# Reciprocal RMS by way of DRAM to all partitions, and the kernel's head written as a function of its own, in a decoder layer on one core

## The chip, the core and the metric

The kernel runs on one core of a Trainium2 chip, as one program. The metric is the device time in microseconds of one execution, the median over runs. A core has TensorE (PE, matmuls; PEld is its weight load), VectorE (DVE), ScalarE (ACT), GpSimd (POOL) and SyncE (SP), each with an instruction stream of its own. DMAs are issued from such a stream and then run on 16 DMA engines. SBUF and PSUM have 128 partitions.

## The reference

One decoder layer over a sequence of 2048 tokens of 1024 features, in float32, cut here to what the change touches:

```python
def rmsnorm(x, w, eps=EPS):
    inv = lax.rsqrt(jnp.mean(x * x, axis=-1, keepdims=True) + eps)   # one number per token
    return x * inv * w

def reference(x, ...):
    proj = rmsnorm(x, norm_mix_w) @ w_in      # k, v, q of attention; f, q, v, g of 4 gated linear-attention heads
    ...                                       # attention in a window of 128 with sinks; chunked recurrence
    h = x + mix @ w_out
    a = rmsnorm(h, norm_ffn_w)
    y = silu(causal_conv(a @ w_gate)) * (a @ w_up)     # 2816 channels
    return rmsnorm(h + y @ w_down, final_norm_w)
```

The inverse 1/rms is one number for each token. It commutes with the matmul, so the kernel multiplies it into the results, not into the input.

## The kernel before

Features lie on partitions and tokens along the free dimension. P is 128, KT = 8 tiles make up the 1024 features, and the sequence is worked in NH = 2 halves of HALF = 1024 tokens. Every float32 matmul is done as three fp32r matmuls of high and low parts (XH by whi, XL by whi, XH by wlo); ACT makes the high part and DVE the low one, for activations (`split`, L215) and weights (`prep`, L177). A `unit` (L190) is one 128-row block of a projection: 8 tiles by 3 products by 2 blocks of 512 tokens, 48 matmuls of 128 x 512 into two PSUM banks. The pool `mm` has four such banks, the pools `hg` and `at` two each.

The stages of a half are: load x and make its parts (`load`, L275); two units `kv` for keys and values (`first_unit`, L306); the unit `f` of the first head; four times a recurrence head (`hgrn`, L433, beginning with its unit `hq`) and an attention head (`attend`, L343), where `att_keys` (L312) multiplies `kv` by the inverse; the output projection (`out_proj`, L646); gate and up in 11 pairs of blocks (`gate_up`, L838), each as seven products of a fast 2 x 2 matrix multiplication with operands S, T and B; and the down projection with the final norm (`down`, L919).

The inverse. `Stats` (L228 on) collects the sum of squares over the feature tiles: ACT squares a tile, DVE adds it to `acc`, 128 x tokens. `inverse` (L243) then sums over partitions with matmuls against a column of ones (`pst`: 8 blocks of 128 tokens, tokens now on partitions) and DVE computes `rs`, 128 x 8, in 13 small steps (`rsqrt`, L155). To have the number of a token on all partitions, `inverse` writes a diagonal matrix (`ident` times `rs`, L253) and `spread` (L257) multiplies it by a matrix of ones (`pinv`, L263, plain f32) and copies the result out of PSUM on ACT (L266). The tile that then holds the inverse is called `invb`, or `sums` for the final norm of half 0. There are nine places: x and h in each half; the final norm of half 0 in two pieces of 512 tokens, s2 and then s1, both worked while half 1's `kv` units run on PE; and that of half 1 in s2 with 512 tokens and two last pieces of 256, whose `pinv` stays in PSUM (`spread(0)`, `spread(1)`).

`finish` (L1089) multiplies eight tiles of the output by the inverse on DVE and stores each. In `gate_up` the inverse of h multiplies the first pair's gate (`ga`, L856), so `then` hangs `hs.inverse` and `hs.spread` on two of that pair's seven products (L865). Behind the multiplies come the convolution (L883, L885) and the next pair's operands.

The head. At the start the first tile of x comes in two parts and the first weight in two column blocks, 128 and 896 wide, with the second weight behind the second tile. The seven small constants are fetched on ACT's queue. PE runs WARM = 12 idle matmuls of ones (L91). Then come `kv` (96 matmuls), the statistics, `f` with the spread hung on its fifth step, and the first `hq`. Loads are issued by SP in program order. The order of instructions on each engine is made by a scheduler, which simulates the program with its own costs and goes by that; program order and the calls of `issue_after` bind it only in part.

Of the kernel before, what the change touches and what calls it, by code (L numbers as in the profile page):

```python
# [13 lines left out]
ALU = mybir.AluOpType  # L14
# [35 lines left out]
def hymba_layer(ctx: ExitStack, tc: tile.TileContext, a: dict, out: bass.AP):  # L50
# [32 lines left out]
    nc.scalar.activation(warm, ones[:, 0:1], AF.Sigmoid)  # L83
# [20 lines left out]
    def constants():  # L104
# [21 lines left out]
        nc.scalar.dma_start(battn, a["b_attn"])  # L126
# [3 lines left out]
        nc.scalar.dma_start(C.hgw, a["hg_norm_w"])  # L130
        C.sinkb = cp.tile([P, ATT_J, 2], F32, name="sinkb")
        nc.scalar.dma_start(C.sinkb.rearrange("p j k -> p (j k)"), a["sinks"].to_broadcast([P, 8]))
        C.nfw = cp.tile([P, KT], F32, name="nfw")
        nc.scalar.dma_start(C.nfw, a["norm_ffn_w"])
        C.fnw = cp.tile([P, KT], F32, name="fnw")
        nc.scalar.dma_start(C.fnw, a["final_norm_w"])
        C.cw = cp.tile([P, FT, 4], F32, name="cw")
        nc.scalar.dma_start(C.cw, a["conv"])

        lbl = cp.tile([P, 2, HG], F32, name="lbl")  # L140
        nc.scalar.dma_start(lbl, a["lb_logits"])
# [35 lines left out]
    def prep(src, slots=False, parts=(slice(0, D),), between=[]):  # L177

        raw = raw4(None)
        hi, lo = [hp.tile([P, D], F32R, tag="m", name=f"w{t}", bufs=KT) if slots else  # L180
                  wp.tile([P, D], F32R, tag=t, name=f"w{t}", bufs=2) for t in ("hi", "lo")]
        for c in parts:
            nc.sync.dma_start(raw[:, c], src[:, c])
            nc.scalar.copy(hi[:, c], raw[:, c])  # L184
            nc.vector.tensor_tensor(lo[:, c], raw[:, c], hi[:, c].bitcast(F32), op=ALU.subtract)  # L185
            if between:
                between.pop(0)()
        return hi, lo

    def unit(src, X, name, order=range(KT), kind="mm", then={}, behind={}, in_turn=False):  # L190
# [5 lines left out]
        for both in [[h] for h in halves()] if in_turn else [halves()]:  # L196
            for i, kt in enumerate(order):
# [6 lines left out]
                with tc.issue_after(mark) if mark else ExitStack():  # L204
                    for w, x, f, l in ((wh, xh, kt == order[0], False), (wh, xl, False, False),
                                       (wl, xh, False, kt == order[-1])):
                        for b, bs in both:
                            nc.tensor.matmul(o[b], w, x[:, bs], start=f, stop=l)  # L208
# [16 lines left out]

    class Stats:


        def __init__(self, acc, sq=None, eng=None, k=0):
            self.acc, self.sq, self.eng, self.k = acc, sq, eng or [nc.vector], k  # L230

        def halves(self):
            n = self.acc.shape[-1] // 2
            return [Stats(self.acc[:, i * n:(i + 1) * n], self.sq, self.eng, self.k) for i in range(2)]

        def add(self, src):
            t = self.acc if self.k == 0 else self.sq()[:, 0:src.shape[-1]] if self.sq else src
            nc.scalar.activation(t, src, AF.Square)
            self.k += 1
            if self.k > 1:  # L240
                return self.eng[(self.k - 1) % len(self.eng)].tensor_tensor(self.acc, self.acc, t, op=ALU.add)

        def inverse(self, keep):  # L243
# [4 lines left out]
            for c in range(nt):  # L248
                nc.tensor.matmul(st[:, c:c + 1], self.acc[:, c * P:(c + 1) * P], ones[:, 0:1],
                                 start=True, stop=True)  # L250
            rs = self.rs = rsqrt(st[:, 0:nt], nt, 1.0 / D, keep)
            dg = self.acc
            return nc.vector.tensor_tensor(dg.rearrange("p (c t) -> p c t", t=P),  # L253
# [3 lines left out]
        def spread(self, bank=None):  # L257

            n = self.acc.shape[-1]
            w = min(n, 512)  # L260
            for b in range(n // w):
                pb = ps(aux[b % 2 if bank is None else bank], "pinv")[:, 0:w]
                nc.tensor.matmul(pb, ones, self.acc[:, b * w:(b + 1) * w], start=True, stop=True)  # L263
                if bank is not None:
                    return pb
                nc.scalar.copy(self.acc[:, b * w:(b + 1) * w], pb)  # L266
# [8 lines left out]
    def load(hf, X, stage, W=None):  # L275

        st = Stats(inv_tile())
        xt = []

        def part(kt, c):  # L280
            nc.sync.dma_start(xt[kt][:, c], a["xT"][kt, :, hf * HALF + c.start:hf * HALF + c.stop])
            split(xt[kt][:, c], nmw[:, kt:kt + 1], dst=[t[:, c] for t in X[kt]])

        for kt in range(KT):
            xt.append(stage())
# [923 lines left out]
```

## Time and profile before

| | us |
|---|---|
| median of 3 runs (2201.37 to 2201.8) | 2201.75 |
| the profiled execution | 2201.32 |
| its span in the profile | 2199.6 |
| PE busy | 2176.4 |
| DVE busy | 1643.6 |
| ACT busy | 1050.3 |
| POOL busy | 6.3 |

Times in the profile are microseconds from the span's start. A row of the timeline has start, duration, engine, line, operation, output<-inputs, shape, and the number of instructions in a group; in brackets stands how long the engine had been idle before it and what it waited for. An f32 matmul of full precision leaves two records on PE. In a table of windows a line has the stretch, its length, then busy time (and instructions) of PE, PEld, DVE, ACT and POOL, the clock that TensorE was granted, the mean busy share of the DMA engines, and what they moved in GB/s.

### The profile page before, as it was taken

What the parts mean: (1) busy time and instruction counts of PE and PEld (TensorE: products, weight loads), DVE (VectorE), ACT (ScalarE), POOL (GpSimd) and SP (SyncE); (2) the same over time, 40 slices, a digit from 0 to 9 for tenths busy, and PEclk for the clock granted to TensorE, in tenths of its full rate; (3) what the DMA queues carried; (4) which work ended last, traced back from release to release, by engine and by line L of the source; (5) the groups of instructions that cost most, each with busy time, mean ns of one, the idle gap of its engine ahead of it and who ended that gap; (6) DMA issues with size and microseconds to landing.
All of it is one profiled execution on the core that took longest, in us unless ns stands there. A gap on an engine that the chain in (4) does not pass through costs nothing.

```text
span 2199.6 us, 29514 instructions
## 1 busy us (share of the span) xinstructions
PE 2176.4 (99%) x11406; PEld 1831.2 (83%) x11406; DVE 1643.6 (75%) x2490; ACT 1050.3 (48%) x1845; POOL 6.3 (0%) x27
## 2 busy tenths in 40 slices
PE   9999999999999999999999999999999999999998
PEld 7988988888888888888889889888888888888887
DVE  6568568688887888875856666577888888887766
ACT  5446454454444445335725455535634444444353
POOL 1000000000000000000000000000000000000000
PEclk9999999999999999999999999999999999999999
DMA  4101112323333234964631111204132323259643
GB/s 154 51 30 50 37 44 68 119 73 104 102 111 106 91 125 144 377 235 162 202 125 49 37 37 50 68 30 139 53 134 87 127 84 120 96 190 392 225 136 130
DMA packets 94214, 257.91 MB, mean 117 GB/s; under 512 B 11578, under 2 KB 17402, under 8 KB 94074
## 3 DMA queue, kind: packets, MB, share of 16 engines
q1 hardware_dynamic: 88128, 251.70, 33.5%
q10 hardware_dynamic: 5946, 4.34, 0.7%
q8 instruction: 89, 1.46, 0.3%
q14 instruction: 51, 0.42, 0.1%
HBM read 195.10 MB, written 57.15 MB: 115 GB/s over the span
## 4 chain that ended last, share of the span: by engine, by line
PE 95%; DVE 3%; DMA 1%; ACT 1%; issue 0%; ACTq 0%; DVEq 0%
PE X L790 7%; PE X L791 7%; PE X L792 7%; PE pop L208 7%; PE hq L208 4%; PE q L208 4%; PE f L208 4%; PE g L208 4%; PE pdx L1001 4%; PE pdx L1003 4%; PE Y L792 4%; PE Y L791 4%; PE Y L790 4%; PE pdx L1002 4%; PE pdy L1003 3%; PE pdy L1001 3%
## 5 line engine op out<-in xcount | busy, mean ns | idle before, releaser
L619 ACT CAST whi<-raw 128x1024 fp32r<-128x1024 f32 x88 | 92.7, 1053 | 109.8 <-PE X L791 67.6
L790 PE MATMUL X<-T,whi 128*128 128x512 f32 x352 | 136.9, 389 | 0.0
L791 PE MATMUL X<-T,whi 128*128 128x512 f32 x352 | 136.9, 389 | 0.0
L792 PE MATMUL X<-T,wlo 128*128 128x512 f32 x352 | 136.9, 389 | 0.0
L885 DVE SCALAR_TENSOR_TENSOR y<-ga,cw,y 128x1024 f32<-128x1024 f32 x88 | 112.4, 1279 | 26.0 <-ACT y L883 25.9
L797 ACT COPY u<-X 128x512 f32<-128x512 f32 x88 | 51.5, 585 | 133.8 <-PE X L792 133.7
L620 DVE TENSOR_TENSOR wlo<-raw,whi 128x1024 fp32r<-128x1024 f32 x88 | 107.1, 1217 | 0.0
L184 ACT CAST whi<-raw 128x1024 fp32r<-128x1024 f32 (+2 forms) x61 | 62.7, 1033 | 81.9 <-PE q L208 31.9
L620 DVE TENSOR_TENSOR xld<-raw,xhd 128x1024 fp32r<-128x1024 f32 x72 | 80.7, 1131 | 19.0 <-ACT xhd L619 18.6
L619 ACT CAST xhd<-raw 128x1024 fp32r<-128x1024 f32 x72 | 69.7, 978 | 42.8 <-DMA raw<-act0T 15.3
L208 PE MATMUL pop<-XL,whi 128*128 128x512 f32 x256 | 85.3, 393 | 2.1 <-DVE XL L220 2.1
L208 PE MATMUL pop<-XH,wlo 128*128 128x512 f32 x256 | 84.6, 391 | 0.8 <-DVE wlo L185 0.8
L208 PE MATMUL pop<-XH,whi 128*128 128x512 f32 x256 | 83.9, 395 | 0.2
L185 DVE TENSOR_TENSOR wlo<-raw,whi 128x1024 fp32r<-128x1024 f32 (+2 forms) x61 | 73.1, 1204 | 8.9 <-ACT whi L184 8.9
L792 PEld LDWEIGHTS X<-T,wlo 128*128 128x128 f32 x352 | 66.1, 188 | 13.7
L791 PEld LDWEIGHTS X<-T,whi 128*128 128x128 f32 x352 | 66.1, 188 | 13.8
L790 PEld LDWEIGHTS X<-T,whi 128*128 128x128 f32 x352 | 66.1, 188 | 13.7
L1001 PE MATMUL pdx<-xhd,hid 128*128 128x512 f32 x192 | 74.4, 391 | 1.2 <-ACT hid L619 1.0
L1002 PE MATMUL pdx<-xld,hid 128*128 128x512 f32 x192 | 74.7, 389 | 0.0
L1003 PE MATMUL pdx<-xhd,lod 128*128 128x512 f32 x192 | 73.7, 389 | 0.0
L611 PE MATMUL pvv<-whi,XH 128*128 128x256 f32 x256 | 73.5, 288 | 0.0
L612 PE MATMUL pvv<-whi,XL 128*128 128x256 f32 x256 | 72.7, 285 | 0.0
(363 smaller groups left out, 6560.8 us busy)
## 6 DMA issues: line engine op xcount, KB each, us to landing
wr<-in_w_down SPq DMA_DIRECT2D x90, 512.0 KB, 5.3
raw<-in_w_gate SPq DMA_DIRECT2D x44, 512.0 KB, 3.6
raw<-in_w_up SPq DMA_DIRECT2D x44, 512.0 KB, 3.6
raw<-act0T SPq DMA_DIRECT2D x20, 512.0 KB, 5.8
raw<-act1T SPq DMA_DIRECT2D x20, 512.0 KB, 10.2
act0B<-y SPq DMA_DIRECT2D x33, 256.0 KB, 2.5
act1B<-y SPq DMA_DIRECT2D x33, 256.0 KB, 2.4
raw<-in_w_out SPq DMA_DIRECT2D x16, 512.0 KB, 4.8
```

Source lines behind the costliest of these rows:

```text
L185: nc.vector.tensor_tensor(lo[:, c], raw[:, c], hi[:, c].bitcast(F32), op=ALU.subtract)
L208: nc.tensor.matmul(o[b], w, x[:, bs], start=f, stop=l)
L611: nc.tensor.matmul(o[:, 0:256], xh[:, t], hi[:, c], start=kt == 0, stop=False)
L619: return (nc.scalar.copy(h, src), (eng or nc.vector).tensor_tensor(l, src, h.bitcast(F32), op=ALU.subtract))
L620: (eng or nc.vector).tensor_tensor(l, src, h.bitcast(F32), op=ALU.subtract))
L790: nc.tensor.matmul(o, wh[:, ws], xh, start=i == 0 and not more, stop=False, skip_group_check=more)
L791: nc.tensor.matmul(o, wh[:, ws], xl, start=False, stop=False, skip_group_check=more)
L792: r = nc.tensor.matmul(o, wl[:, ws], xh, start=False, stop=i == 3, skip_group_check=more)
L885: nc.vector.scalar_tensor_tensor(y, g[:, w:w + HALF], C.cw[:, ft, w:w + 1], y, op0=ALU.mult, op1=ALU.add)
L1001: nc.tensor.matmul(o, wh[:, i, c], ah[:, i, cols], start=f, stop=False, skip_group_check=more)
L1002: nc.tensor.matmul(o, wh[:, i, c], al[:, i, cols], start=False, stop=False, skip_group_check=more)
L1003: nc.tensor.matmul(o, wl[:, i, c], ah[:, i, cols], start=False, stop=l, skip_group_check=more)
```

## The change

Seven of the nine inverses (x and h of both halves, s2 of half 0, s1, and the 512-token s2 of half 1) no longer use the diagonal, the matrix of ones and the copies. `inverse` with `sent` writes `rs` to a row in DRAM by a DMA from ACT's queue, tokens in order, and a second DMA, from POOL's queue, reads that row onto every one of the 128 partitions of `acc`: 1024 or 512 numbers on each. The last two pieces of 256 tokens keep the matrix of ones (`sent=False`).

The head becomes a function. `head` gives ACT's instructions an order (`turn`) and PE's likewise, step by step: `step(u, kt)` is one feature tile of one of the two kv units, six matmuls. The first weight is loaded in column blocks of 128, 384 and 512, the last two from ACT's queue ahead of the warm-up activation, and cast in these blocks; the second is cast in blocks of 256 and 768, and its first two steps come before x's third tile. x's tiles are all requested one behind the other, without a wait for the weights' casts. The constants are fetched from SP's queue, behind the loads of x and of `w_f`. The weights of `f` are cast before the statistics, and `f` stands behind `pst` on PE. The scheduler's order changes as well in the later stages, among them that of the products of the first gate and up pairs.

```diff
+        def inverse(self, keep, sent=True):
 
             n = self.acc.shape[-1]
             nt = n // P
             st = ps("hg", "pst")
             for c in range(nt):
-                nc.tensor.matmul(st[:, c:c + 1], self.acc[:, c * P:(c + 1) * P], ones[:, 0:1],
+                marks["pst"] = nc.tensor.matmul(st[:, c:c + 1], self.acc[:, c * P:(c + 1) * P], ones[:, 0:1],
                                  start=True, stop=True)
             rs = self.rs = rsqrt(st[:, 0:nt], nt, 1.0 / D, keep)
+            if sent:
+                row = dp.tile([nt, P], F32, name=f"row{len(sent_rows)}")
+                sent_rows.append(row)
+                nc.scalar.dma_start(row.rearrange("c p -> p c"), rs)
+                nc.gpsimd.dma_start(self.acc, row.rearrange("c p -> (c p)").unsqueeze(0).to_broadcast([P, n]))
+                return
             dg = self.acc
-            return nc.vector.tensor_tensor(dg.rearrange("p (c t) -> p c t", t=P),
+            nc.vector.tensor_tensor(dg.rearrange("p (c t) -> p c t", t=P),
                                     ident.unsqueeze(1).to_broadcast([P, nt, P]),
                                     rs.unsqueeze(2).to_broadcast([P, nt, P]), op=ALU.mult)
 
-        def spread(self, bank=None):
+        def spread(self, bank):
 
             n = self.acc.shape[-1]
-            w = min(n, 512)
-            for b in range(n // w):
-                pb = ps(aux[b % 2 if bank is None else bank], "pinv")[:, 0:w]
-                nc.tensor.matmul(pb, ones, self.acc[:, b * w:(b + 1) * w], start=True, stop=True)
-                if bank is not None:
-                    return pb
-                nc.scalar.copy(self.acc[:, b * w:(b + 1) * w], pb)
+            pb = ps(aux[bank], "pinv")[:, 0:n]
+            nc.tensor.matmul(pb, ones, self.acc, start=True, stop=True)
+            return pb
...
+    def head(X):
+
+
+        st = Stats(inv_tile())
+        raw = [raw4(None) for _ in range(3)]
+        W = [tuple(wp.tile([P, D], F32R, tag=t, name=f"w{t}", bufs=2) for t in ("hi", "lo")) for _ in range(2)]
+        xt = [slot("x") for _ in range(KT)]
+        k0, k1, k2 = slice(0, P), slice(P, 4 * P), slice(4 * P, D)
+        v0, v1 = slice(0, 2 * P), slice(2 * P, D)
+        nc.sync.dma_start(raw[0][:, k0], a["w_att"][ATT_J][:, k0])
+        for c in (k1, k2):
+            fetched = nc.scalar.dma_start(raw[0][:, c], a["w_att"][ATT_J][:, c])
+        with tc.issue_after(fetched.ins):
+            nc.scalar.activation(warm, ones[:, 0:1], AF.Sigmoid)
+        for kt in range(KT):
+            for c in [h for _, h in halves()] if kt == 0 else [slice(0, HALF)]:
+                nc.sync.dma_start(xt[kt][:, c], a["xT"][kt, :, c])
+            if kt == 1:
+                nc.sync.dma_start(raw[1], a["w_att"][ATT_J + 1])
+        nc.sync.dma_start(raw[2], a["w_f"][0])
+        o = [[ps("mm", f"kv{b}") for b in range(NB)] for _ in range(2)]
+        on_act, on_pe = [], []
+
+        def turn(f, *args):
+
+            with tc.issue_after(on_act[-1].ins) if on_act else ExitStack():
+                on_act.append(f(*args))
+
+        def tile_of_x(kt):
+            X.append(new_x())
+            for c in [h for _, h in halves()] if kt == 0 else [slice(0, HALF)]:
+                turn(split_w, xt[kt][:, c], nmw[:, kt:kt + 1], [t[:, c] for t in X[kt]])
+
+        def split_w(src, w, dst):
+            h, l = dst
+            r = nc.scalar.activation(h, src, AF.Identity, scale=w)
+            nc.vector.scalar_tensor_tensor(l, src, w, h.bitcast(F32), op0=ALU.mult, op1=ALU.subtract)
+            return r
+
+        def step(u, kt):
+
+            hi, lo = [t[:, kt * P:(kt + 1) * P] for t in W[u]]
+            xh, xl = X[kt]
+            with tc.issue_after(on_pe[-1].ins) if on_pe else ExitStack():
+                for w, x, f, l in ((hi, xh, kt == 0, False), (hi, xl, False, False), (lo, xh, False, kt == KT - 1)):
+                    for b, bs in halves():
+                        r = nc.tensor.matmul(o[u][b], w, x[:, bs], start=f, stop=l)
+                on_pe.append(r)
+
+        turn(cut, *W[0], raw[0], k0)
+        tile_of_x(0)
+        step(0, 0)
+        turn(cut, *W[0], raw[0], k1)
+        tile_of_x(1)
+        step(0, 1)
+        turn(cut, *W[0], raw[0], k2)
+        turn(cut, *W[1], raw[1], v0)
+        for kt in range(2):
+            step(1, kt)
+        for kt in range(2, KT):
+            tile_of_x(kt)
+            if kt == 2:
+                turn(cut, *W[1], raw[1], v1)
             else:
-                part(kt, slice(0, HALF))
-            if W is not None and kt == 1:
-                W.append(prep(a["w_att"][ATT_J + 1]))
-
-            if W is None:
-                st.add(xt[kt])
-            elif kt >= 3:
-                st.add(xt[kt - 3])
-            yield st
-        for kt in range(KT - 3, KT) if W is not None else ():
-            st.add(xt[kt])
-
-    def first_unit(X, W, i, then={}):
-        return unit(W[i] if W else a["w_att"][ATT_J + i], X, "kv", then=then)
+                turn(st.square, xt[kt - 3])
+            for u in range(2):
+                step(u, kt)
+        F = tuple(hp.tile([P, D], F32R, tag="m", name=f"w{t}", bufs=KT) for t in ("hi", "lo"))
+        turn(cut, *F, raw[2], slice(0, D))
+        for kt in range(KT - 3, KT):
+            turn(st.square, xt[kt])
+        summed = st.last
+        with tc.issue_after(on_act[-1].ins), tc.issue_after(summed.ins):
+            constants()
+        with tc.issue_after(on_pe[-1].ins):
+            st.inverse("x")
+        with tc.issue_after(marks["pst"].ins):
+            f0 = unit(F, X, "f", kind="aux")
+        return o, st.acc, st.rs, f0, summed
+
+    def first_unit(X, i, then={}):
...
-            then = {"S4": lambda: hs.inverse("h"), "A22": lambda: (hs.spread(), flush())} if pr == 0 else {}
+            then = {"S4": lambda: hs.inverse("h"), "A22": flush} if pr == 0 else {}
...
-                        steps[0][0].inverse("o")
+                        steps[0][0].inverse("o", False)
                     elif i and d == 1:
                         inv = steps[0][0].spread(0)
                     elif i and d == 2:
                         finish(hf, hh, steps[0][0], steps[0][1], [nc.sync], inv)
-            steps[1][0].inverse("o")
+            steps[1][0].inverse("o", False)
             finish(hf, hh, steps[1][0], steps[1][1], [nc.scalar, nc.sync], steps[1][0].spread(1))
             return None
-        kv = [first_unit(X, None, 0, {3: lambda: s1.inverse("o"), 7: lambda: xs.inverse("x")})]
-        kv.append(first_unit(X, None, 1, {2: lambda: (s1.spread(), finish(hf, hh, s1, lo, [nc.sync])), 4: xs.spread}))
+        kv = [first_unit(X, 0, {3: lambda: s1.inverse("o"), 7: lambda: xs.inverse("x")})]
+        kv.append(first_unit(X, 1, {2: lambda: finish(hf, hh, s1, lo, [nc.sync])}))
...
-    X, W = [], []
-    for xs in load(0, X, lambda: slot("x"), W):
-        pass
-    kv = [first_unit(X, W, i) for i in range(2)]
-    constants()
-    xs.inverse("x")
-    f0 = unit(a["w_f"][0], X, "f", kind="aux", then={4: xs.spread})
-    nxt = X, kv, xs.acc, xs.rs, f0
+    X = []
+    *nxt, summed = X, *head(X)
...
-        nc.scalar.dma_start(battn, a["b_attn"])
+        nc.sync.dma_start(battn, a["b_attn"])
-        nc.scalar.dma_start(lbl, a["lb_logits"])
+        nc.sync.dma_start(lbl, a["lb_logits"])
```

More of the change, by code (lines that the diff above doesn't have):

```diff
@@ L272, in slot, with load @@
         return hp.tile([P, HALF], F32, tag="m", name=name, bufs=KT)
[L275 removed]
+    def load(hf, X, stage):
         st = Stats(inv_tile())
[L278 to L282, printed above, removed]
         for kt in range(KT):
[L285 removed]
+            x = stage()
             X.append(new_x())
[L287 to L304 removed]
@@ L1113, in hymba_layer @@
                 at = attend(hf, h, X, invb, KS, V, mix, p)
-                next(hg)
+                with tc.issue_after(summed.ins) if hf + h == 0 else ExitStack():
+                    next(hg)
                 if h == HG - 1:
```

59 lines of the change are left out of this document (30 added, 29 removed).

## The prediction

> **What bounds the kernel now.** I read the page's busy shares first, then the chain that ended last, then the windows by stage.
>
> ```profile
> PE 2176.4 (99%) x11406; PEld 1831.2 (83%) x11406; DVE 1643.6 (75%) x2490; ACT 1050.3 (48%) x1845; POOL 6.3 (0%) x27
> PE 95%; DVE 3%; DMA 1%; ACT 1%; issue 0%; ACTq 0%; DVEq 0%
> 10.00:13.00 3.00, 2.18 (x6) 1.38 (x6) 2.03 (x2) 2.68 (x3) 0.00 (x0) 0.50 1.03 404
> 13.00:16.00 3.00, 3.00 (x9) 2.32 (x8) 2.49 (x4) 3.00 (x4) 0.00 (x0) 0.50 1.03 407
> 17.00:20.00 3.00, 3.00 (x15) 2.48 (x14) 3.00 (x3) 2.97 (x5) 0.00 (x0) 1.00 1.02 407
> 600.00:1100.00 500.00, 499.49 (x2208) 413.35 (x2207) 399.51 (x480) 239.33 (x311) 0.00 (x0) 1.00 0.49 171
> ```
>
> PE is busy 99% of the span and is 95% of the chain. The windows have, after the stretch's length, the busy time of PE, PEld, DVE, ACT and POOL, then the granted clock, the DMA engines' busy share and GB/s. From 600 to 1100 PE idles 0.5 of 500 us, so an instruction taken from PE there shortens the span by its own time, and later work on another engine costs nothing until PE lacks an operand. Only the first 17 us differ: PE has holes, and its granted clock is 0.50 from 10 to 16. So the change has two sides: what it takes from PE, and whether PE must wait for what comes instead. The profiled execution took 2201.32 us (span 2199.6 and 1.72 around it), 0.02% under the median of 2201.75; I sum against 2201.32.
>
> **The ones-matmuls that go.** Beside the tile summary of `pinv` (duration min/median/max), PE's timeline shows what one costs:
>
> ```profile
> L263 PE MATMUL pinv<-invb,ones x22: 379/592/796, 44.9 to 2192.8; 128*128 128x512 f32 x18, 128*128 128x256 f32 x4
> L263 PE MATMUL pinv<-sums,ones x4: 590/590/591, 1102.1 to 1118.4; 128*128 128x512 f32 x4
> 44.02 0.62 PE L208 MATMUL f<-XH,whi 128*128 128x512 f32 x2
> 44.47 0.62 PE L208 MATMUL f<-XL,whi 128*128 128x512 f32 x2
> 44.93 1.88 PE L263 MATMUL pinv<-invb,ones 128*128 128x512 f32 x4
> 46.24 1.04 PE L208 MATMUL f<-XH,wlo 128*128 128x512 f32 x2
> 47.12 0.62 PE L208 MATMUL f<-XH,whi 128*128 128x512 f32 x2
> 48.50 0.39 PE L208 MATMUL hq<-XH,whi 128*128 128x512 f32 x1
> ```
>
> Pairs of matmuls start every 0.45 us (44.02, 44.47), 0.227 each. After the pair at 44.47 the next two should start at 44.93 and 45.38; with four `pinv` records (two matmuls; an f32 one is two records) the second starts at 47.12. So two cost 47.12 − 45.38 = 1.73 us, one 0.87. Of 26 records 22 have 512 columns, which are 11 matmuls: two each for x and h in both halves, and one each for the final norm's s2 of half 0, s1, and s2 of half 1. All 11 go; the last two eighths keep theirs (four records of 256 columns). 11 × 0.87 = **−9.5 us**, all where PE is the chain. The diagonals on DVE and the copies of `pinv` on ACT go too; they lie beside PE and count nothing.
>
> **The new trip.** Now rs goes from ACT's queue to a DRAM row, 1024 or 512 elements of 4 bytes, and from POOL's queue back to 128 partitions, 512 or 256 KB. The second waits for the first. Before has neither, and no DMA on POOL's queue. The nearest rows (issue to landing):
>
> ```profile
> DMA to landing us min/median/max: 1.8/2.5/4.2
> raw<-in_w_gate SPq DMA_DIRECT2D x44, 512.0 KB, 3.6
> wr<-in_w_down SPq DMA_DIRECT2D x90, 512.0 KB, 5.3
> raw<-act1T SPq DMA_DIRECT2D x20, 512.0 KB, 10.2
> ```
>
> The first row is that of `odd<-moved`, a small DMA on ACT's queue. Call L the time from rs to the landed broadcast. It is at least 1.8 + 3.6 = 5.4 and at most 4.2 + 10.2 = 14.4. I take 2.5 + 5.3 = 7.8, say 8: a weight load is nearest in size, and the slower of the weight rows allows for a queue that nothing used before. The Trainium skill's page "DMA: Bandwidth & Descriptors", section "Anatomy of one DMA — SWDGE (gpsimd) path", gives such a DMA 2.0 us plus its bytes at 436 GB/s, an estimated 3.2 us for 512 KB; with the 2.5 in front L would be 5.7, no site below would wait, and the sum would be −12.0. No run here shows a DMA of that queue.
>
> What L may be before PE waits, site by site. **x of half 0:**
>
> ```profile
> 34.02 1.84 PE L249 MATMUL pst<-ones,invb 128*128 128x1 f32 x16
> 38.43 0.17 DVE L168 SCALAR_TENSOR_TENSOR y<-t,y 128x8 f32<-128x8 f32 x1
> 46.60 0.69 DVE L326 TENSOR_TENSOR kT<-kv,invb 128x512 f32<-128x512 f32 x1 [6.67 <-ACT invb L266]
> ```
>
> The key/value units end at 33.8, rs 4.8 later at 38.60; in the new order the last sum of squares comes some 0.5 us later against them, so 5.3. Then PE has pst (1.84) and f, 48 × 0.227 = 10.9, until 12.8 after the units' end. hq then needs a PSUM bank that kT's multiply frees, 0.7 after the landing. PE waits 5.3 + L + 0.7 − 12.8 = L − 6.8: **+1.2 us** at L = 8, nothing up to 6.8, 7.6 at 14.4. The row's DMA also holds ACT until rs is there; behind it stands kT's activation, which needs the inverse anyhow.
>
> **h, twice.** The inverse meets the first gate pair:
>
> ```profile
> 484.71 0.17 DVE L168 SCALAR_TENSOR_TENSOR y<-t,y 128x8 f32<-128x8 f32 x1
> 488.68 2.50 DVE L856 TENSOR_TENSOR ga<-ga,invb 128x512 f32<-128x512 f32 x4 [2.55 <-ACT invb L266]
> 494.90 1.05 ACT L619 CAST Sh<-S 128x1024 fp32r<-128x1024 f32 x1
> 500.56 0.39 PE L790 MATMUL Y<-T,Sh 128*128 128x512 f32 x1
> ```
>
> The multiplies start 3.8 us after rs; behind them on DVE and ACT stand the convolution and the next pair's operands, of which Sh is ready at 495.95 and read at 500.56. That is 4.6 us of slack, less the 1.7 by which PE comes earlier, less 1.2 for Sl's subtract that follows Sh; and in PE's new order 20 more matmuls stand before that read, 4.5 us. PE waits from L = 3.8 + 4.6 − 1.7 − 1.2 + 4.5, about 10: nothing at 8. DVE's new order puts two subtracts (1.9 us) ahead of the multiplies; they fit in its 2.55 us of idle time. On ACT behind the row stand copies of X and Y that wait for PE until 487 anyway, after rs.
>
> **x of half 1, with s1:**
>
> ```profile
> 1112.77 1.22 DVE L253 TENSOR_TENSOR invb<-ident,y 128x1024 f32<-128x1024 f32 x1
> 1122.39 0.39 PE L208 MATMUL f<-XH,whi 128*128 128x512 f32 x1
> 1124.46 1.28 DVE L326 TENSOR_TENSOR kT<-kv,invb 128x512 f32<-128x512 f32 x2
> ```
>
> rs is there at 1112.7. f starts 3 × 0.87 earlier plus the one of s2, near 1119, and ends near 1130: L ≤ 11 is covered (1112.7 + 11 + a multiply of s1 in front and kT's own, some 5, is 1129). Nothing at 8. Behind ACT's row of s1 stands a weight cast, whose load is there long before.
>
> **Tail, s2 of half 1:**
>
> ```profile
> 2163.13 0.16 DVE L168 SCALAR_TENSOR_TENSOR y<-t,y 128x4 f32<-128x4 f32 x1
> 2167.45 4.91 DVE L1092 TENSOR_TENSOR h<-h,invb 128x512 f32<-128x512 f32 x8
> 2172.28 0.41 DVE L987 TENSOR_TENSOR h<-h,pdx 128x256 f32<-128x256 f32 x1
> 2176.70 0.50 PE L249 MATMUL pst<-ones,invb 128*128 128x1 f32 x4
> ```
>
> Eight multiplies of 4.91 stand on DVE ahead of the last sums, of which the pst at 2176.70 needs all. They could start 2163.3 + L instead of 2167.45; the sums behind them take till about 4.9 after that, pst can wait until L ≈ 7.8. **+0.2** at 8. Its row has half the bytes, which is on the safe side. The end (last pst, last `pinv`, four multiplies, store) is untouched.
>
> **The head.** Constants leave ACT's queue for SP's, behind w_f and ahead of the next weights; ACT, DVE and PE get a step order by hand.
>
> ```profile
> 9.41 0.33 ACTq L141 DMA_DIRECT2D lbl<-in_lb_logits  x1
> 32.85 2.00 ACT L184 CAST whi<-raw 128x1024 fp32r<-128x1024 f32 x2 [5.60 <-PE kv L208]
> 7.98 0.49 PE L208 MATMUL kv<-XH,whi 128*128 128x512 f32 x1 [0.36 <-ACT XH L222]
> 9.15 0.60 PE L208 MATMUL kv<-XL,whi 128*128 128x512 f32 x1 [0.68 <-DVE XL L223]
> 9.79 1.15 ACT L222 ACTIVATE XH<-x,nmw 128x1024 fp32r<-128x1024 f32 x1 [0.92 <-DMA sinkb<-in_sinks]
> 10.97 1.28 DVE L223 SCALAR_TENSOR_TENSOR XL<-x,nmw,XH 128x1024 fp32r<-128x1024 f32 x1 [1.88 <-ACT XH L222]
> 10.99 2.16 PE L208 MATMUL kv<-XH,whi 128*128 128x512 f32 x4 [0.82 <-ACT XH L222]
> ```
>
> Seven issues of 0.33 are 2.3 us that SP's later loads wait; those are cast after 33, twenty us after their old issue, so this costs nothing; without that cover it would be the 2.3. Before, ACT sits behind a constant's DMA until 9.79, and PE has its second x tile at 10.99. Played through with the durations above, XH of x1 comes at 8.7, XL at 10.0, the first two tiles are done at 13.6 for both units, and six more take 12 × 0.227 = 2.7 each (DVE's 2.5 per tile fits): units end at 29.9 instead of 33.8, **3.9** less. That is at full clock. A half-clock stretch of 3 us, as from 10 to 13, costs half of it, 1.5; both stretches 3. I count one, **−2.5**, and keep 0.9 to 3.9 as its ends. The Trainium skill, "TensorE: Matmul & The Clock Gate", Part 1, has the clock halve after an idle window of some 3.4 us that runs freely; the trace agrees with a half clock after the holes, for some 6 us. By that rule the gain hangs on where a window falls.
>
> Sum: −9.5 − 2.5 + 1.2 + 0.2 = −10.6, so **2190.7 us**.
>
> **Rivals.** The window of the first site:
>
> ```profile
> 36.00:50.00 14.00, 14.00 (x59) 10.83 (x58) 6.88 (x21) 3.74 (x6) 0.00 (x0) 1.00 0.21 75
> ```
>
> *A slow trip.* As L grows, all sites charge: gain = 12.0 − (L − 6.8) − (L − 7.8) − 2(L − 10) − (L − 11), each bracket from its own zero. At 10 it is 6.6, at 11 2.6, at 11.6 nothing, at 13 −7.4: **2208.7, slower**. It decides from L = 12.5 on, which costs over 0.2% (4.4 us, about what a measurement of this kernel can tell from no change). For it: act1T's 10.2 us, a store of 1024 single elements, 128 reads of one 4 KB row, a queue never seen here. Against it: at these places the DMA engines are idle for 79% of the time from 36 to 50, and the weight loads land in 3.6 to 5.3. I give 0.13, and 0.10 to L from 10.7 to 12.5, which lands within 0.2%.
>
> *POOL's transfer held by DVE.* If its descriptors wait until DVE pauses, it starts later by one DVE instruction, 1.2 to 2.5 us by the subtracts above: L = 10, gain 6.6, **2194.7**. Against it: DVE is idle 6.67 us at the first site, and busy 6.88 of 14 us around it. Chance 0.09. The Trainium skill, "SBUF — State Buffer", section "SBUF: two separate sides", says that a DMA issued from GpSimd starves while DVE runs a two-port fast-mode operation, with 620 ns grown to 3100; no run here shows it.
>
> *The head brings nothing.* The kernel's first tiles come when the loads land, and PE falls into the same half clock. Then units end as before, the waits of 1.4 stay: 2201.32 − 9.5 + 1.4 = **2193.2**. For it: the loads already ran at 404 GB/s from 10 us on. Chance 0.13. That the change does not do what it says would be `pinv` records at 45 us; the new order has none there.
>
> **Numbers.** The forecast (L from 5.4 to 9.5, head 0.9 to 3.9) has 0.55; with the last two rivals faster has **0.77**, same **0.10**, slower **0.13**. Its own range is 2187.9 (12.0 + 1.4 gained, no wait) to 2195. Downward 1.9 more for what the scheduler's new order of the gate and up products may save (the size of those two subtracts); upward I go into the slow trip as far as L ≈ 11.6: 2186 to 2201.3, with some 0.16 above it and 0.04 below.
>
> **What would show it.** Right: no L263-like f32 matmul between 40 and 2170; units ending between 30 and 33; the broadcast landing 7 to 9 us after the last y; PE idle about 1 us before the first hq; the first gate pair without idle PE. Wrong: a broadcast landing over 11 us after rs, with PE idle before hq, before the second gate pair and before the tail's pst; or units ending at 33.8 again at a half clock.

## The result and the profile after

| | us |
|---|---|
| before, median of 5 runs (2200.27 to 2201.8) | 2201.37 |
| changed, median of 5 runs (2238.2 to 2244.3) | 2241.18 |
| ratio, 95% interval | 1.0184, 1.0172 to 1.0195 |
| forecast | 2190.7, 2186.0 to 2201.3 |

The change makes the kernel 39.8 us slower. The changed kernel's page, in the rows that answer to those of before (busy shares, chain), and its two small DMA queues:

```profile
PE 2172.0 (97%) x11384; PEld 1829.2 (82%) x11384; DVE 1636.2 (73%) x2485; ACT 1044.7 (47%) x1836; POOL 9.8 (0%) x34
PE 85%; DMA 6%; DVE 6%; ACT 1%; issue 1%; SPq 0%; DVEq 0%; POOLq 0%; ACTq 0%
q10 hardware_dynamic: 10970, 4.75, 0.8%
q0 software_dynamic: 816, 2.88, 0.4%
```

PE has 22 records fewer, as forecast, and is busy only 4.4 us less; of the span of 2236.3 it idles 64.3 us, against 23.2 of 2199.6 before. DMA has become 6% of the chain. What PE waits for (engine, line, waited for: us, times, longest):

```profile
PE pv L407 <- ACT vT L398: 13.7, 1, 13.7
PE pst L252 <- DVE invb L239: 9.1, 2, 7.0
PE Y L861 <- ACT Sh L690: 8.8, 2, 5.5
PE hq L203 <- DVE kT L397: 7.9, 1, 7.9
```

Those are the forecast's own sites: x of half 1, the tail, the first gate pair of both halves, x of half 0. Here is the earliest of them, x of half 0, in the timeline, then the windows (stretch, length, busy PE, PEld, DVE, ACT, POOL, granted clock, DMA share, GB/s):

```profile
35.81 0.17 DVE L167 SCALAR_TENSOR_TENSOR y<-t,y 128x8 f32<-128x8 f32 x1
36.01 0.39 ACTq L258 DMA_DIRECT2D row<-y  x1
47.25 0.70 POOL L259 DMA_DIRECT2D invb<-row  x1 [40.69 <-DMA row<-y]
51.05 1.29 DVE L397 TENSOR_TENSOR kT<-kv,invb 128x512 f32<-128x512 f32 x2 [15.08 <-DMA invb<-row]
51.89 0.77 PE L203 MATMUL hq<-XH,whi 128*128 128x512 f32 x1 [7.85 <-DVE kT L397]
```

```profile
36.00:38.00 2.00, 2.00 (x11) 1.65 (x10) 0.00 (x0) 0.00 (x0) 0.00 (x0) 1.00 0.46 94
38.00:40.00 2.00, 2.00 (x10) 1.68 (x9) 0.00 (x0) 0.00 (x0) 0.00 (x0) 1.00 0.00 0
42.00:44.00 2.00, 2.00 (x10) 1.35 (x8) 0.00 (x0) 0.00 (x0) 0.00 (x0) 1.00 0.00 0
52.00:56.00 4.00, 4.00 (x11) 3.18 (x12) 2.81 (x5) 3.95 (x6) 0.00 (x0) 0.60 0.00 0
```

The store of rs is issued at 36.01, and the broadcast that waits for it at 47.25: 11.2 us for 4 KB. The broadcast then needs 3.8 from its issue. The DMA engines are busy only until 38; the packet records of ACT's queue in the trace end at 37.68, and the store's 16 semaphore updates come from 44.67 to 46.65. So the bytes have left after 1.7 us; for the next seven nothing moves and nothing is reported, and the updates then take two more. L, the time from rs to the landed broadcast, is 51.05 − 35.98 = 15.1. And after the wait PE works at a clock of 0.60 (52 to 56).

The other six stores take as long, those of 512 numbers as much as those of 1024. Four of them:

```profile
491.09 0.40 ACTq L258 DMA_DIRECT2D row<-y  x1
502.97 0.53 POOL L259 DMA_DIRECT2D invb<-row  x1 [455.02 <-DMA row<-y]
1108.17 0.37 ACTq L258 DMA_DIRECT2D row<-y  x1
1118.06 0.54 POOL L259 DMA_DIRECT2D sums<-row  x1 [614.56 <-DMA row<-y]
1131.17 0.37 ACTq L258 DMA_DIRECT2D row<-y  x1
1144.15 0.53 POOL L259 DMA_DIRECT2D invb<-row  x1 [2.55 <-DMA row<-y]
1599.37 0.39 ACTq L258 DMA_DIRECT2D row<-y  x1
1608.78 0.53 POOL L259 DMA_DIRECT2D invb<-row  x1 [464.10 <-DMA row<-y]
```

From the store's issue to the broadcast's that is 11.9, 9.9 (512 numbers), 13.0 and 9.4 us; for the two not shown, s1 and the tail (512 each), it is 11.4 and 10.5. All seven lie between 9.4 and 13.0.

### The profile page after: what moved, and what is told of

Read it like the earlier page. It is cut to its first block, busy times and chain, and to the rows that moved or that the text cites. A ratio compares the mean times of both kernels' runs of the same rounds, so it can differ in the third digit from the quotient of the medians.

```text
span 2236.3 us, 29435 instructions
## 1 busy us (share of the span) xinstructions
PE 2172.0 (97%) x11384; PEld 1829.2 (82%) x11384; DVE 1636.2 (73%) x2485; ACT 1044.7 (47%) x1836; POOL 9.8 (0%) x34
## 4 chain that ended last, share of the span: by engine, by line
PE 85%; DMA 6%; DVE 6%; ACT 1%; issue 1%; SPq 0%; DVEq 0%; POOLq 0%; ACTq 0%
PE pop L203 7%; PE X L861 7%; PE X L862 7%; PE X L863 7%; PE hq L203 4%; PE q L203 4%; PE g L203 3%; PE Y L861 3%; PE Y L862 3%; PE Y L863 3%; PE pdx L1072 3%; PE pdx L1074 3%; PE pdx L1073 3%; DMA row<-y 3%; PE f L203 3%; PE pdy L1072 3%
## 5 line engine op out<-in xcount | busy, mean ns | idle before, releaser
L690 ACT CAST whi<-raw 128x1024 fp32r<-128x1024 f32 x88 | 92.2, 1050 | 82.0 <-PE X L862 51.5
L181 ACT CAST whi<-raw 128x1024 fp32r<-128x1024 f32 x57 | 59.4, 1047 | 91.2 <-PE q L203 31.9
L861 PE MATMUL Y<-T,Sh 128*128 128x512 f32 x176 | 69.3, 394 | 8.8 <-ACT Sh L690 8.8
L868 ACT COPY s<-X 128x512 f32<-128x512 f32 x44 | 25.8, 586 | 101.0 <-PE X L863 101.0
```

The lines of the kernel that those rows point to most:

```text
L690: return (nc.scalar.copy(h, src), (eng or nc.vector).tensor_tensor(l, src, h.bitcast(F32), op=ALU.subtract))
L861: nc.tensor.matmul(o, wh[:, ws], xh, start=i == 0 and not more, stop=False, skip_group_check=more)
L868: copied[:] = [nc.scalar.copy(t, o)]
```

## The experiments

Ratios are against the kernel before in the same call (2200.4 to 2202.1).

**The head alone.** The rows are taken out of the changed kernel; the diagonals and ones-matmuls are back at all places.

```diff
-        def inverse(self, keep, sent=True):
+        def inverse(self, keep, sent=False):
...
-            f0 = unit(F, X, "f", kind="aux")
+            f0 = unit(F, X, "f", kind="aux", then={4: st.spread})
```

> The new head with the old inverses (diagonal and matrix of ones at all nine places). Theory: the head's part of the change is right as the changed kernel's trace shows it, with the key/value units ending at 31.2 instead of 33.8; the rest of the kernel is as before: 2201.4 - 2.6 = 2198.8, ratio 0.9988. Rival: the scheduler's other order or the later statistics eat it, ratio 0.9995 to 1.001.

Measured 2197.77, ratio 0.9986 (0.9978 to 0.9995). In its timeline the `kv` units end, and `pst` begins, here instead of at 34.02:

```profile
31.16 1.84 PE L252 MATMUL pst<-ones,invb 128*128 128x1 f32 x16
```

The head is worth 2.9 us in the trace (34.02 − 31.16) and 3.0 by the medians, in its place and about the size expected.

**The rows alone,** in the head of before (`inverse` of the change put into the kernel before, its `spread` calls taken out).

> The old head with the seven rows by DRAM. Theory: all the loss lies in the rows, so the changed kernel's time plus the head's 2.6: 2241.2 + 2.6 = 2243.8, from 2238 to 2248. Rival (the new head's order on the engines makes the waits longer): under 2235.

Measured 2245.45, ratio 1.0206 (1.0192 to 1.022). All the loss is in the rows.

**Another order of the stored numbers.** One edit, in the changed kernel: each partition's eight (or four) numbers go out in one run. The broadcast then has the inverses at other tokens than their own, so this kernel computes something else and serves for its time alone.

```diff
-                row = dp.tile([nt, P], F32, name=f"row{len(sent_rows)}")
+                row = dp.tile([P, nt], F32, name=f"row{len(sent_rows)}")
...
-                nc.scalar.dma_start(row.rearrange("c p -> p c"), rs)
+                nc.scalar.dma_start(row, rs)
```

> The changed kernel, with rs stored as it lies, 32 or 16 bytes from each partition in one run, in place of single elements put into the order of tokens; the row is read as before. The inverses then stand at other tokens. Theory A (single elements are what is slow): the store lands after 2.5 us, the broadcast 4.4 later, L about 7; PE waits some 0.2 us before hq and nowhere else: 2201.4 - 9.5 - 2.6 + 0.2, 2189.5, from 2187 to 2194. Theory B (any store read back takes this long): as the changed kernel, 2236 to 2245.

Measured 2189.55, ratio 0.995 (0.9935 to 0.9965). Its page and first site:

```profile
PE 2161.9 (99%) x11384; PEld 1823.8 (83%) x11384; DVE 1637.4 (75%) x2485; ACT 1045.4 (48%) x1836; POOL 9.9 (0%) x34
35.96 0.34 ACTq L258 DMA_DIRECT2D row<-y  x1
38.47 0.70 POOL L259 DMA_DIRECT2D invb<-row  x1 [31.91 <-DMA row<-y]
42.56 1.29 DVE L397 TENSOR_TENSOR kT<-kv,invb 128x512 f32<-128x512 f32 x2 [6.63 <-DMA invb<-row]
```

The store now takes 2.5 us in place of 11.2, the broadcast is as before, L is 6.6, and PE waits nowhere for one of the seven inverses. The same bytes, queues, waits and instruction counts: the whole 51.6 us between this run and the changed kernel hang on where the 4-byte numbers lie in the row, and with it on whether they go out one by one or in runs. The pages of the two profiled executions, 49.5 us apart, show how they divide. PE's idle time falls from 64.3 to 24.9 (2186.8 − 2161.9), 39.4 us; and the same 11384 records take PE 2161.9 instead of 2172.0, another 10.1 us. Most of that is the lower clock behind the waits. In the changed kernel the granted clock is 0.50 from 48.3 to 55.2, 512.6 to 516.0, 1147.4 to 1161.1, 1618.5 to 1621.9 and 2209.0 to 2215.8, each time from within a wait to some us behind it. In this run no such stretch is left; in both the clock is low at the very end. An estimate from these records, busy time by one minus the clock, gives a loss of 9.4 us in the changed kernel and 0.6 here.

**Stores by themselves.** Into the kernel before, eight stores that nothing reads. A first run had them all at the start:

> The kernel before, with eight small stores of a constant added, one in each recurrence head, away from the path (nothing reads them). Time from issue to the last semaphore update is what counts. Theory A (a store of single 4-byte elements to DRAM is confirmed late): the row of 8 x 128 single elements lands after 9 to 11 us, the one of 4 x 128 after 5 to 10, the same 1024 numbers in 128 runs of 32 bytes after 2 to 3, in 8 runs of 512 bytes after 2 to 2.5, and single elements into SBUF after 2 to 3. If it is elements of one DRAM line that hinder each other, single elements 512 bytes apart land after 2 to 4 us; if it is the number of single writes, they also take 9 to 11, and 128 of them take about 3. Theory B (any store to DRAM is confirmed that late when little else moves): all stores to DRAM land after 9 to 11 us, the one into SBUF after 2 to 3. Theory C (ACT's queue): the row from SP's queue lands after 2 to 3 us, that from ACT's after 10. Time of the kernel: 2201 to 2203.

The kernel took 2210.59. The scheduler put the stores between 11 and 30 us, among the first loads and upon each other, so no landing can be read from it; that eight small stores, 26.5 KB in all, went with 9.8 us in that place is all it says, and it is one run. The next two runs took a fresh result of each head as the source, which set them some 80 us apart:

```diff
+                done = [k for k in range(KT) if mix[k] is not None]
+                probe(hf * HG + h, mix[done[-1]])
```

> The eight stores once more, now each from a result that the head just computed, so that they come some 80 us apart, out of the start's traffic (the kernel before otherwise; nothing reads the stores). Theory A (single 4-byte elements to DRAM are confirmed late): 1024 of them in the order of tokens land 9 to 11 us after the issue, from SP's queue too; 1024 in 128 runs of 32 bytes and 8 runs of 512 bytes after 2 to 3; 1024 single elements into SBUF after 2 to 3. Within A, if the elements of one DRAM line hinder each other: single elements 512 bytes apart after 2 to 4, and 512 elements in 4 rows as long as 1024 (9 to 11); if each single write costs: apart 9 to 11, 512 elements about 6, 128 about 3. Theory B (every store): all to DRAM 9 to 11. Theory C (ACT's queue): SP's row 2 to 3.

> The kernel before with stores of 1024 single 4-byte elements in the order of tokens, with 8, 16, 32, 64, 128 and 256 bytes from one element to the next, one store in each head; then 128 runs of 16 bytes, and the row without gaps again. If elements are hindered by others in the same small line, the landing falls with the number in a line and is short (2.7 us, as with 512 bytes) from one spacing on; a line of 64 bytes would show as 10, 8, 5 and then 2.7 us from 64 bytes on. If what counts is the whole span of the row (4 KB), it falls smoothly to 512. Runs of 16 bytes: 1.5 to 2.5 us. The row again: 9 to 11.

The times of the kernels, one run each, are 2203.51 and 2206.95. From the trace's packet and semaphore records, us from the issue of a store, and what else the DMA engines moved in the 6 us behind it:

| stored to DRAM unless said | last packet ends | last update | others, MB |
|---|---|---|---|
| 1024 single numbers, no gap (8 rows of 512 bytes) | 6.3 | 10.0 | 0.44 |
| the same in the second run | 1.6 | 10.9 | 0 |
| the same from SP's queue | 1.6 | 9.8 | 0 |
| 512 of them (4 rows) | 12.7 | 13.1 | 0.41 |
| 128 of them (1 row) | 1.1 | 7.9 | 0 |
| 1024 single, 8 bytes from one to the next | 4.9 | 5.6 | 0.45 |
| 16 bytes | 5.1 | 5.9 | 0.53 |
| 32 bytes | 1.6 | 2.7 | 0 |
| 64 bytes | 1.6 | 2.6 | 0.02 |
| 128 bytes | 3.1 | 4.0 | 0.45 |
| 256 bytes | 3.3 | 4.0 | 0.52 |
| 512 bytes | 1.6 | 2.7 | 0.02 |
| 128 runs of 32 bytes | 1.1 | 1.5 | 0 |
| 128 runs of 16 bytes | 1.1 | 1.4 | 0 |
| 8 runs of 512 bytes | 2.0 | 3.0 | 0.45 |
| 1024 single into SBUF | 3.3 | 3.6 | 0.52 |

(From SP, in the second run's repeat and for the 8 runs of 512 bytes, nine of the sixteen updates are on record.) Theory B and the queue are out: stores to DRAM that leave gaps or go in runs land in 1.4 to 5.9, and SP's row is as slow as ACT's. Neither the number of elements nor their size is what costs: 1024 single numbers land in 2.7 us when each has 32 bytes to itself, and 128 without gaps need 7.9. From 32 bytes on, and for runs, the landing follows the last packet by 0.3 to 1.1 us. Without gaps, and with nothing else moving, it comes 6.8 to 9.3 us behind it (rows two, three and five). So it is single numbers laid close together that are confirmed late, and 32 bytes apart is enough; the expected figure was 64.

What happens between 4 and 32 bytes stays open. At 8 and 16 bytes the landing follows the last packet by 0.7 and 0.8 us; the packets end late there, but both stores ran beside loads of half a megabyte, and so did the 128 and 256 bytes (3.1 and 3.3), so that the lateness can't be put to the distance alone. Nor is it shown that numbers hinder each other by sharing 32 bytes: the 128 runs of 16 bytes share them in twos and land in 1.4. What works behind the packets can't be seen here. But a transfer beside such a store can be late too. Here is the load of 512 KB that ran beside the 512 numbers without gaps, and then the one beside the 16 bytes (KB, us to landing):

```profile
raw<-in_w_f SPq DMA_DIRECT2D x1, 512.0 KB, 12.8
raw<-in_w_f SPq DMA_DIRECT2D x1, 512.0 KB, 5.1
```

Elsewhere in the two traces such a load lands in 3.4 to 3.6. In the run of the rows alone one broadcast of 256 KB, with another such store under way, took 9.6.

**Runs in the right order, by strided sums.** `pst` sums every 8th (4th) token, so that neighbouring tokens share a partition.

```diff
-                marks["pst"] = nc.tensor.matmul(st[:, c:c + 1], self.acc[:, c * P:(c + 1) * P], ones[:, 0:1],
+                tokens = self.acc[:, c::nt] if sent else self.acc[:, c * P:(c + 1) * P]
+                marks["pst"] = nc.tensor.matmul(st[:, c:c + 1], tokens, ones[:, 0:1],
...
+                    self.rs = sp.tile([P, nt], F32, tag="rsx", name="rsx")
+                    nc.scalar.dma_start(self.rs, tokens.rearrange("(c p) -> p c", p=P))
```

> The changed kernel with the sums taken over every 8th (or 4th) token, so that a partition holds neighbouring tokens and its 32 (16) bytes go out in one run in the right order; for x a small DMA from ACT's queue reads rs back in the old layout, which later work needs. Theory: as the run with runs of 32 bytes, L about 6.6 and no waits: 2189 to 2190, ratio 0.995. Rival (the strided weight loads of the column sums, or ACT held for the small read, cost): 2191 to 2195.

Measured 2220.74, ratio 1.0087 (1.0073 to 1.01): neither. The trip is short (POOL's broadcast at 39.2 behind a store at 37.2), and PE doesn't wait, but is busy 2193.7 us. The sums' summary (duration min/median/max) of the run in other order and of this one, and this one's clock behind the first sums:

```profile
L252 PE MATMUL pst<-ones,invb x80: 164/251/251, 31.1 to 2176.2; 128*128 128x1 f32 x80
```

```profile
L253 PE MATMUL pst<-ones,invb x80: 164/376/378, 31.0 to 2207.3; 128*128 128x1 f32 x80
31.00:35.00 4.00, 4.00 (x19) 3.90 (x19) 2.38 (x7) 2.24 (x3) 0.00 (x0) 0.97 0.60 152
35.00:38.00 3.00, 3.00 (x9) 2.32 (x8) 1.87 (x14) 0.00 (x0) 0.00 (x0) 0.50 0.40 150
```

A weight tile read at a stride of 32 bytes takes PE longer (from the start of each `pst` record to the next start on PE it has 23.3 us in place of 13.1), and a clock of 0.50 follows for some 3 us though PE was never idle. A third part was not foreseen: all matmuls of gate and up started every 229.8 ns, not 226.7. Two runs went on from there.

> The run with strided column sums (2220.7) once more, with x's rs read back into the tile that it was stored from instead of a new one of 32 bytes per partition. In that run the matmuls of gate and up started every 229.8 ns on average instead of 226.7. If the new tile's shift of all later tiles did that, they start every 226.7 again and the time is 3.1 ns x 3700 = 11.5 us less, 2209, from 2206 to 2213. If it is the strided loads that slow them, it stays at 2217 to 2222.

Here the small read goes back into the tile that rs was stored from:

```diff
-                    self.rs = sp.tile([P, nt], F32, tag="rsx", name="rsx")
-                    nc.scalar.dma_start(self.rs, tokens.rearrange("(c p) -> p c", p=P))
+                    nc.scalar.dma_start(rs, tokens.rearrange("(c p) -> p c", p=P))
```

Measured 2206.64, ratio 1.0025 (1.0016 to 1.0034), and 226.7 ns again. So 14.1 us went with a tile of 32 more bytes per partition ahead of all later tiles. The broadcast from SP below has that tile too and starts a matmul every 229.7 ns; every other kernel here is without it, strided sums or not, and at 226.7. That it is the shift of the later tiles is argued from these; which property of their place counts is not shown. The strided sums' rest is still there:

```profile
35.00:38.00 3.00, 3.00 (x11) 2.71 (x12) 1.45 (x12) 0.14 (x1) 0.00 (x0) 0.57 0.86 289
```

> As the runs in order, but x in both halves again by the diagonal and the matrix of ones (four ones-matmuls of 512 columns back on PE, 4 x 0.87). Theory (PE's time is what counts and nothing waits): 3.5 us slower than the runs in order, 2192.5 to 2193.5. Rival (the trip for x of half 0 costs a wait before hq that the matrix does not): only 1 to 2.5 slower.

With x by ones (`xs.inverse("x", False)` and `xs.spread` back), measured 2205.34, ratio 1.0016 (1.0007 to 1.0026). The figure expected had the wrong base, since the other places keep strided sums; against the run above with the normal cadence it is 1.3 less, which the two intervals don't tell from nothing: four ones-matmuls come (3.5), x's strided sums and their low clock go. It does not tell the two theories apart. It does show where the low clock comes from: there is none here behind the sums of x in half 0, which are not strided, and there is 0.50 from 471.0 to 477.8 behind h's strided ones, with PE busy throughout. In the run in other order, whose sums are not strided, the clock stays at 1.00 at both places. (Such a stretch can also come without strided sums or a wait: the kernel before has one of 3.4 us at 1456.7.)

> As the run before with the broadcast issued from SP's queue in place of POOL's. Theory (the issuing queue matters little): the broadcast lands 3.3 to 4 us after its issue as from POOL (4.0), the time within 1 us of the run before. Rival (POOL's way of issuing is the slower): 1 us shorter landing, no change of the time since no site waits. Rival (SP's loads behind the waiting broadcast come late): 1 to 6 us slower.

With `nc.sync` for `nc.gpsimd` in the broadcast, measured 2218.34, ratio 1.0074 (1.0061 to 1.0088), within the interval of its base. In its timeline:

```profile
39.22 0.34 ACTq L259 DMA_DIRECT2D row<-y  x1
40.69 0.33 SPq L261 DMA_DIRECT2D invb<-row  x1
44.09 1.29 DVE L402 TENSOR_TENSOR kT<-kv,invb 128x512 f32<-128x512 f32 x2 [4.91 <-DMA invb<-row]
```

From the store's issue to kT it takes 4.9 us (the same steps from POOL: 6.4), and no site cares. POOL's queue is 1.5 us slower here and not at fault.

**Runs in the right order, without strided loads.** ACT writes the squares of h and the final norm in the order that is wanted; x's rs is turned by PE.

```diff
-            r = nc.scalar.activation(t, src, AF.Square)
+            if self.perm:
+                r = nc.scalar.activation(t.rearrange("q (c p) -> q p c", c=4),
+                                         src.rearrange("q (p c) -> q p c", c=4), AF.Square)
...
+            turned = self.st[0:nt, P:2 * P]
+            marks["turned"] = nc.tensor.matmul(turned, self.rs, ident, start=True, stop=True)
+            nc.scalar.copy(self.acc[0:nt, 0:P], turned)
+            nc.scalar.dma_start(row, self.acc[0:nt, 0:P])
...
-            f0 = unit(F, X, "f", kind="aux")
+            f0 = unit(F, X, "f", kind="aux", then={2: st.send}, behind={2: "turned"})
```

> The changed kernel with stores in runs and the right order, without strided weight loads: for h and the final norm ACT writes its squares with every fourth token together, so that a partition's rs are of neighbouring tokens and go out in runs of 16 bytes; for x, whose rs is needed in the old layout, PE turns rs (128 x 8) by a small matmul with the identity after 12 matmuls of f, ACT copies it, and it goes out in runs of 512 bytes. Theory: 9.5 and 2.6 less than before, plus 0.2 for each of two small matmuls and 0.1 to 1.4 of waiting before hq: 2201.4 - 12.1 + 0.4 + 0.5 = 2190.2, from 2189 to 2191.5. Rival (ACT's scattered writes are slower, or the small matmul's wait holds PE): 2192 to 2197.

Measured 2191.73, ratio 0.9956 (0.9943 to 0.9968), 9.7 us under the kernel before and 49 under the changed one; it lies 0.2 above the range expected and just under that of the other outcome. Its page and first site:

```profile
PE 2163.8 (99%) x11388; PEld 1823.9 (83%) x11388; DVE 1638.4 (75%) x2485; ACT 1070.6 (49%) x1838; POOL 9.9 (0%) x34
36.23 0.38 PE L280 MATMUL pst<-ident,y 128*8 128x128 f32 x2 [0.24 <-DVE y L167]
36.64 0.26 ACT L281 COPY invb<-pst 8x128 f32<-8x128 f32 x1 [3.06 <-PE pst L280]
36.93 0.54 ACTq L282 DMA_DIRECT2D row<-invb  x1
38.73 0.70 POOL L283 DMA_DIRECT2D invb<-row  x1 [32.16 <-DMA row<-invb]
42.65 1.29 DVE L416 TENSOR_TENSOR kT<-kv,invb 128x512 f32<-128x512 f32 x2 [6.57 <-DMA invb<-row]
```

The detour costs 0.9 us from rs to the store's issue, the store 1.8, and hq is not held. ACT is busy 26 us more (its scattered squares), off the path.

> As the run before, with x in both halves by the diagonal and the matrix of ones. Theory: four ones-matmuls of 0.87 us back, the small matmuls and the wait gone: 2201.4 - 2.6 - 7 x 0.87 = 2192.7, 2 to 3 us more than the run before. Rival (x's trip in half 0 still costs a wait of 3 us): no more than the run before.

With x by ones: 2195.43, ratio 0.9972 (0.9962 to 0.9982), 3.7 us more than the run before, though the two intervals overlap; four ones-matmuls at 0.87 are 3.5, and two small turning matmuls go. That fits the price of a `pinv` put back, where nothing waits.

## Why the prediction was wrong

- **What bounds the kernel.** Right: PE, through all of it.
- **Ones-matmuls, −9.5.** Right. The run in other order gained 11.2 by the medians and the head alone 3.0, which leaves 8.2 (9.2 by the two profiled spans, 2196.0 and 2186.8), and the last run prices four at about 3.7.
- **The new trip, L about 8, at most 14.4.** This is the step that failed, in its first term. The store was priced by `odd<-moved`, 1.8 to 4.2 us, taken at 2.5; it took 9.4 to 13.0, and L was 14 to 17 at the places where PE waits. The second term (5.3, with 3.6 to 10.2 for its ends) was safe: the broadcast needed about 4. The row chosen was of a DMA within SBUF in long runs; "a store of 1024 single elements" stood only in the rival's reasons, without a price, and single elements into SBUF would have been no warning either (3.6). The Trainium skill's rule of 2.0 us plus the bytes at 436 GB/s, which the prediction weighed ("DMA: Bandwidth & Descriptors", section "Anatomy of one DMA — SWDGE (gpsimd) path"), speaks of a DMA from POOL's queue and came near there: an estimated 3.2 for 512 KB, against 3.8 to 4.2 measured from issue to landing in the changed kernel.
- **The sites.** Right in place, and close in size at three of the four when the measured L is put in. x of half 0: 15.1 − 6.8 = 8.3, measured 7.9. h: 507.02 − 489.97 = 17.1 and so 7.1, measured 5.5. The tail: 14.0 − 7.8 = 6.2, measured 7.0. Mis-sized was x of half 1, with 5.9 (L 16.9) against 13.7:

```profile
1122.46 4.91 DVE L1161 TENSOR_TENSOR h<-h,sums 128x512 f32<-128x512 f32 x8 [9.99 <-DMA sums<-row]
1130.97 0.17 DVE L167 SCALAR_TENSOR_TENSOR y<-t,y 128x8 f32<-128x8 f32 x1
1131.25 0.73 PE L203 MATMUL f<-XH,whi 128*128 128x512 f32 x2
1145.76 4.90 DVE L1161 TENSOR_TENSOR h<-h,sums 128x512 f32<-128x512 f32 x8 [13.31 <-DMA sums<-row]
1156.52 1.12 PE L407 MATMUL pv<-ident,vT 128*128 128x128 f32 x4 [13.75 <-ACT vT L398]
```

Two things were missing in its sum. The first is the trip of s2, which the sum has no site for. Its eight multiplies stand on DVE ahead of the steps that make rs of s1 and of x, and DVE idles 9.99 us for its row (2.89 in the run in other order). So x's rs is there at 1131.14, with f only beginning on PE; the working had rs at 1112.7 and f at 1119, some 6 us of cover more. The second lies behind the landing, at 1148.04. kT has to wait for s1's multiplies, which run until 1150.66, and it is not hq that stands next on PE but `pv`, which needs vT, and vT has two casts in front of it on ACT. From the landing to `pv` that is 8.5 us, where the working allowed some 5.
- **The slow trip as a rival.** The right mechanism, with 0.13. Its sum at L = 15 is 2218.7, with 29.4 us of waits; the traced execution took 2238.2, 19.5 more. PE waited 37.4 at the sites, 8 more and nearly all of it at x of half 1, and PE's busy time was 10.1 longer, for which the sum had no term. About 1.4 is left over.
- **The head, −2.5.** Right in the sum (2.9 measured), in part by luck: two misses nearly cancel. The clock is at 1.00 throughout the new head, so the 1.5 for a half-clock stretch was not to be taken off. But the second tile of x is ready a microsecond later than worked out, XH at 9.70 and XL at 11.01 instead of 8.7 and 10.0, because ACT waits for that tile's load until 8.55 (the last line is a window, with its clock of 1.00):

```profile
8.55 1.15 ACT L332 ACTIVATE XH<-x,nmw 128x1024 fp32r<-128x1024 f32 x1 [0.67 <-DMA x<-in_xT]
9.73 1.28 DVE L333 SCALAR_TENSOR_TENSOR XL<-x,nmw,XH 128x1024 fp32r<-128x1024 f32 x1 [1.00 <-ACT XH L332]
9.00:13.00 4.00, 2.71 (x11) 1.91 (x11) 2.90 (x4) 3.39 (x6) 0.00 (x0) 1.00 1.03 417
```

The prediction also put the half clock of the old head down to PE's holes. The traces don't show that: those that it listed last 0.82 us at most, and the new head has holes of up to 1.05 us at a clock of 1.00. What set the half clock there stays open.
- **POOL's transfer held by DVE.** Not settled. The 512 KB broadcasts of the changed kernel landed 3.8 to 4.2 us after their issue, and 1.5 us is all that another queue saved, but no run changes what DVE does meanwhile.

## What to carry to other kernels

Price a DMA by a row with the same run length and the same target: a few KB of single numbers, packed into DRAM, were confirmed some 7 to 9 us after their packets had gone, and runs of 16 bytes or more 1.4 to 3.0 us after their issue. The cheapest repair is to arrange the numbers on the engines, so that a partition holds neighbours, and not with strided weight loads. Where the time of a trip is uncertain, work out the cover of every site first, as here: the sites told at once which waits had come true, and a store with L = 6.6 fitted under all of them. Then follow each engine's order from site to site: one late row kept DVE from making the next.

## What the runs showed of the hardware

Single 4-byte writes to DRAM without gaps had their last semaphore update after 7.9 to 13.1 us, where nothing else moved 6.8 to 9.3 us behind the last packet's record; 32 bytes and more apart it came after 2.6 to 4.0 us, at 8 and 16 bytes, beside other traffic, after 5.6 and 5.9, and for runs of 16 to 512 bytes after 1.4 to 3.0. A 512 KB load beside 512 such writes without gaps took 12.8 us, against 3.4 to 3.6 elsewhere in these traces. A weight load with a stride of 32 bytes took 0.376 us a record against 0.251, and a granted clock of 0.50 followed sixteen of them for 3 to 7 us, with PE busy. And a tile of 32 bytes per partition more in SBUF went with 229.8 and 229.7 ns in place of 226.7 from matmul to matmul in a whole stage.
